# A hybrid trunk layer on one core: new costs and a new waiting rule in the model that orders the projection stage

## The chip, the cores and the metric

One core of a Trainium2 chip runs the whole layer as one program. The metric is the device time of one execution in microseconds (us), from a few repeated runs; smaller is better. The engines are TensorE (PE in the profile: matmul, with its weight loads as PEld), VectorE (DVE), ScalarE (ACT), GpSimd (POOL) and SyncE (SP, which here only issues transfers).

## The reference, cut to what matters

The input is one sequence of 512 frames with 1024 channels. The layer normalizes it, multiplies it by one wide input matrix, and feeds the columns to two recurrent token mixers of eight heads each, which are merged and added back; then an expert retrieval follows, which the change does not touch.

```python
h = _rmsnorm(x, norm1[l])
proj = h @ w_in[l]
a_q, a_k, a_v, a_beta, a_alpha, a_gate, b_f, b_i, b_q, b_gate, g_a, g_b = _split_cols(proj)
...
o_a = _gated_delta_rule(qa, ka, va, beta, log_alpha)
o_a = _rmsnorm(o_a, a_onorm[l]) * jax.nn.silu(a_gate.astype(f32)).reshape(bsz, t, A_HEADS, A_DV)
y_a = o_a.reshape(bsz, t, A_V).astype(dt) @ w_branch_a[l]
...
o_b = _hgrn2_recurrence(qb, 1.0 - f_gate, ib, jnp.log(f_gate))
o_b = _rmsnorm(o_b, b_onorm[l]) * jax.nn.sigmoid(b_gate.astype(f32)).reshape(bsz, t, B_HEADS, B_DV)
y_b = o_b.reshape(bsz, t, B_V).astype(dt) @ w_branch_b[l]
mix = jax.nn.sigmoid(g_a) * y_a + jax.nn.sigmoid(g_b) * y_b
x = x + mix @ w_out[l]
```

Branch A (gated DeltaNet) inverts one triangular 128x128 matrix for each head and each of four chunks; branch B (HGRN2) builds its decayed attention matrix level by level. Both carry a state from chunk to chunk.

## The kernel before, in words

**Units.** The input matrix is cut into units of 128 output columns. A unit is 24 matmuls of 512 columns: eight blocks of the contraction, and for each block three products, since both operands are split into a high and a low float32r part (`piece`: `whi*hhi`, `wlo*hhi`, `whi*hlo`). The high part of the weights is made by ScalarE (L265, tile `whi`), the low part by GpSimd (L470, tile `wlo`, a subtraction of 128x1024 elements that reads two tiles in SBUF). `order` lists the units head by head, with eight kinds for each head (a_k, a_q, b_q, a_v, b_f, b_i, b_gate, a_gate) and some units of the merge gates among them. The first five are done ahead of the stage in question; the next 73 are its projections. After a unit's matmuls `consume` turns it into what the branches need: the causal convolution on VectorE (L922, three taps of 511, 510 and 509 columns), gates (L932, L938, L949), a scan (L940).

**Branches.** Four more generators share the stage with the projections. `setup` runs once. `branch_a1` prepares a head of branch A: it normalizes and transposes keys and queries, makes `LT` (L651) and `AT`, scales keys on GpSimd (`kG` L674, `kd` L675), and inverts 16x16 blocks in 15 small steps on GpSimd (L691, L693). `branch_a2` finishes the inverse on TensorE (`iv`), carries the state and writes `ogA` (L803). `branch_b` runs seven levels for each head; a level is one subtraction of 512 columns on VectorE (L822, tile `z`), two exponentials of 256 columns on ScalarE, two products of 256 columns on VectorE (L826, L827), and then matmuls from `z` into `pl`: in each of the first five levels 16 of them, 640 in all for eight heads. The next level's `z` is written out ahead of a level's matmuls.

**What sets the order.** Every engine carries out its instructions in the order in which the program writes them. In this stage that order is made when the program is built. Each generator stops at a `yield` ahead of a TensorE step and names the tiles that the step reads or writes; the projections stop after each block of three matmuls. A class `Flow` keeps a clock for each engine: after each step `note` goes through the instructions just written, and for each one takes the engine's clock, the time at which its inputs are ready (plus a constant for the pair of engines, `wait`) and the time at which its output buffer is free; the end is that start plus `cost`, a duration by engine, operation and size. The loop then takes the step that could start first on TensorE:

```python
when = max(when, flow.pe()) + BIAS[ch[2]]
if best is None or when < best[0]:
    best = when, ch
```

`BIAS` favours `setup` by 600 ns, `branch_a2` by 100 and `branch_a1` by 50; `branch_b` and the projections have none. So a branch step that the model holds to be ready goes first, and one that it holds to be late lets three projection matmuls go ahead of it. The model decides nothing but this order. On the chip the engines wait for each other by semaphores, whatever the model held. Projections may run ahead of a branch by two heads at most (`allowed`), since the buffers of each kind are two.

After the stage two more merge-gate units and the units of the branch matrices follow in a fixed order, then the expert retrieval.

Of the kernel before, what the change touches and what calls it, by code (L numbers as in the profile page):

```python
# [11 lines left out]
F32R = mybir.dt.float32r  # L12
# [8 lines left out]
PSUM = bass.MemoryType.PSUM  # L21
# [113 lines left out]
class Flow:  # L135


    def __init__(self, nc):
        self.nc, self.pos = nc, 0
        self.eng, self.ready, self.used, self.slots, self.last = {}, {}, {}, {}, {}  # L140
        self.dma, self.ln = 0.0, False

    def keys(self, ap):

        if hasattr(ap, "bass_ap"):
            ap = ap.bass_ap
        elif not hasattr(ap, "tensor"):
            return []
        if ap.tensor.space != bass.MemoryType.SB or not hasattr(ap.tensor, "tag"):
            return [(ap.tensor.name, 0)]  # L150
        dims = [list(d) for d in ap.ap]
        lo = ap.offset % dims[0][0] if dims[0][0] else ap.offset
        hi = lo + sum(max(d[0], 0) * (d[1] - 1) for d in dims[1:])
        return [(ap.tensor.name, q) for q in range(lo // 128, hi // 128 + 1)]

    def cost(self, ins, e, op):
        out = ins.outs[0].bass_ap
        n = out.free_size()
        src = ins.ins[0].bass_ap if len(ins.ins) and hasattr(ins.ins[0], "bass_ap") else out
        psum = any(getattr(a.bass_ap, "space", None) == PSUM for a in ins.ins if hasattr(a, "bass_ap"))  # L160
        if e == "PE":
            w = ins.ins[1].bass_ap
            m = w.free_size()
            if src.dtype == F32:
                if ins.is_transpose:
                    return 112
                return 2 + 0.84 * max(m, n) if n <= 64 and m <= 64 else max(215, 4 * n / 2.4)
            return max(n / 2.4, m * (0.84 if src.dtype == F32R else 0.42)) + 3
        if e == "Activation":
            return 51 + 0.833 * n + (90 if psum else 0)  # L170
        if e == "DVE":
            r = 0.75 if op in ("TensorCopy",) else 1.04
            if src.dtype in (BF16, F16) and out.dtype in (BF16, F16):
                r = 0.53
            return 67 + r * n + (58 if psum else 0)
        if e == "Pool":
            if "pow" in str(ins):
                return 958
            return 100 + {"TensorCopy": 3.45, "TensorScalarPtr": 4.5, "Memset": 0.9}.get(op, 2.05) * n
        return 60  # L180

    def note(self):
        ins_list = self.nc.cur_bb.bb.instructions
        for ins in ins_list[self.pos:]:
            e = str(ins.engine).split(".")[-1]
            if not len(ins.outs) or not hasattr(ins.outs[0], "bass_ap"):
                continue
            t = self.eng.get(e, 0.0)
            ins_k = [k for ap in ins.ins for k in self.keys(ap)]
            out_k = [k for ap in ins.outs for k in self.keys(ap)]  # L190
            for k in ins_k:
                if k in self.ready:
                    r, re = self.ready[k]
                    if r + self.wait(re, e) > t:
                        t = r + self.wait(re, e)
            for ap in ins.outs:
                ten = ap.bass_ap.tensor
                tag = getattr(ten, "tag", None)
                if tag is not None:
                    seen = self.slots.setdefault(tag, [])  # L200
                    if ten.name not in seen:
                        seen.append(ten.name)
                        b = ten.tag_meta.bufs
                        if len(seen) > b and self.last.get(seen[-1 - b], 0.0) + 150 > t:
                            t = self.last[seen[-1 - b]] + 150
            for k in out_k:
                if self.used.get(k, 0.0) > t:
                    t = self.used[k]
            op = str(ins.opcode).split(".")[-1]
            if "DMA" in op:  # L210
                self.eng[e] = t + 60
                n = ins.outs[0].bass_ap.nbytes
                n = n() if callable(n) else n
                self.dma = max(self.dma, t + 1100) + n / 360.0
                end = self.dma
                w = "dma"
            else:
                end = t + self.cost(ins, e, op)
                if op == "Activation" and str(ins.func).split(".")[-1] in ("Ln", "Exp", "Tanh"):
                    ln = str(ins.func).endswith("Ln")  # L220
                    end += 1283 * (ln != self.ln)
                    self.ln = ln
                self.eng[e] = end
                w = e
            for k in out_k:
                self.ready[k] = end, w
            for k in ins_k + out_k:
                self.used[k] = max(self.used.get(k, 0.0), end)
                self.last[k[0]] = max(self.last.get(k[0], 0.0), end)
        self.pos = len(ins_list)  # L230
# [1564 lines left out]
```

## Time and profile before

| | us |
|---|---|
| median of three runs | 2124.62 |
| the three runs | 2121.92, 2124.62, 2127.04 |
| the profiled execution, device time | 2124.58 |
| its span, first to last instruction | 2122.8 |
| PE busy | 2043.1 |
| DVE busy | 1452.4 |
| ACT busy | 937.3 |
| POOL busy | 1160.5 |

The span is what the trace covers. Times below are counted from its start. In this trace a matmul's record is longer than its turn on the engine, since matmuls are pipelined; turns are read from the number of matmuls in a stretch. A float32 matmul leaves two records, a float32r or bfloat16 one leaves one. A row of the view of waits gives the total time that an engine stood idle for another one, the number of such waits and the longest.

### The profile page before, as it was taken

Reading aid. Unit: us, or ns where it says so; the run is one execution under the profiler, and the core shown is the slowest. Engines: PE = TensorE matmul, PEld = TensorE weight load, DVE = VectorE, ACT = ScalarE, POOL = GpSimd, SP = SyncE. Lnnn points to the kernel's source line nnn. Section 1 sums busy time; section 2 is a strip of 40 time slices with the busy share of each in tenths; the row PEclk is TensorE's granted clock in tenths of the full one; section 3 lists DMA queues with packets and bytes.
Section 4 is the critical chain, followed back from the end, with each engine's and each line's share of the span. In section 5 each row is a group of like instructions: output and inputs, shape, how many; then the busy total and the mean of one; then the engine's idle time right before and its main releaser. Section 6 shows DMA issues by size and latency. Waiting matters only on the chain. (4 is left out here: it accounts for less than half of the span.)

```text
span 2122.8 us, 34908 instructions
## 1 busy us (share of the span) xinstructions
PE 2043.1 (96%) x13210; PEld 1753.1 (83%) x13210; DVE 1452.4 (68%) x2779; ACT 937.3 (44%) x1742; POOL 1160.5 (55%) x957
## 2 busy tenths in 40 slices
PE   7899999999999999999789999999999999999997
PEld 5678787787787888889778999999999999999776
DVE  7666646556653366999996666676666676666897
ACT  5555555555554323666575333333333333333233
POOL 3556645655654644211101666666667666666787
PEclk9999999999999999999999999999999999999999
DMA  3313132221212543678799988889888888888775
GB/s 132 116 57 111 52 97 72 82 76 62 92 61 92 198 153 129 184 199 199 195 344 315 322 305 302 303 291 317 298 303 304 291 304 311 304 298 287 246 263 211
DMA packets 189463, 439.44 MB, mean 207 GB/s; under 512 B 26960, under 2 KB 90608, under 8 KB 187632
## 3 DMA queue, kind: packets, MB, share of 16 engines
q1 hardware_dynamic: 95248, 230.75, 31.8%
q0 software_dynamic: 42912, 156.26, 23.5%
q10 hardware_dynamic: 51136, 50.22, 7.1%
q8 instruction: 103, 1.69, 0.3%
q14 instruction: 64, 0.52, 0.1%
HBM read 375.81 MB, written 39.34 MB: 196 GB/s over the span
## 5 line engine op out<-in xcount | busy, mean ns | idle before, releaser
L470 POOL TENSOR_TENSOR wlo<-wraw,whi 128x1024 fp32r<-128x1024 f32 x204 | 501.5, 2458 | 304.3 <-ACT whi L265 296.8
L262 PE MATMUL h<-hhi,wlo 128*128 128x384 f32 x1024 | 347.0, 339 | 6.9 <-DMA wlo<-wraw 6.8
L262 PE MATMUL h<-hhi,whi 128*128 128x384 f32 x1024 | 347.7, 340 | 2.8 <-ACT hext L265 2.8
L262 PE MATMUL h<-hlo,whi 128*128 128x384 f32 x1024 | 346.6, 339 | 1.5 <-POOL hlo L435 1.1
L262 PE MATMUL mm<-hhi,whi 128*128 128x512 f32 x792 | 330.3, 417 | 0.0
L262 PE MATMUL mm<-hlo,whi 128*128 128x512 f32 x792 | 312.4, 394 | 4.2 <-POOL hlo L435 3.0
L1686 DVE TENSOR_TENSOR wl<-hg,wh 128x384 fp32r<-128x384 f32 x126 | 129.7, 1029 | 269.2 <-ACT wh L265 251.2
L262 PE MATMUL mm<-hhi,wlo 128*128 128x512 f32 x792 | 310.6, 392 | 0.7 <-POOL wlo L470 0.7
L265 ACT ACTIVATE whi<-wraw 128x1024 fp32r<-128x1024 f32 (+1 forms) x251 | 263.4, 1049 | 106.4 <-PE mm L262 52.3
L262 PE MATMUL y<-vh,wl 128*128 128x512 f32 x756 | 298.7, 395 | 0.6 <-DVE wl L1686 0.6
L262 PE MATMUL y<-vh,wh 128*128 128x512 f32 x756 | 295.1, 390 | 3.1 <-ACT wh L265 3.1
L262 PE MATMUL y<-vl,wh 128*128 128x512 f32 x756 | 297.1, 393 | 0.9 <-POOL vl L1687 0.9
L1609 POOL DMA_INDIRECT row<-eu,eidx x128 | 158.5, 1239 | 145.6 <-DVE stage L1615 130.7
L1609 POOL DMA_INDIRECT row<-ev,eidx x128 | 161.2, 1260 | 126.1 <-DVE stage L1623 101.2
L265 ACT ACTIVATE hext<-h 128x384 f32<-128x384 f32 x88 | 43.1, 490 | 375.7 <-PE h L262 374.5
L262 PEld LDWEIGHTS h<-hhi,wlo 128*128 128x128 f32 x1024 | 193.7, 189 | 12.3 <-DMA wlo<-wraw 8.4
L262 PEld LDWEIGHTS h<-hhi,whi 128*128 128x128 f32 x1024 | 193.7, 189 | 7.5 <-ACT hext L265 3.5
L262 PEld LDWEIGHTS h<-hlo,whi 128*128 128x128 f32 x1024 | 193.6, 189 | 2.4 <-POOL hlo L435 1.8
L1623 DVE SCALAR_TENSOR_TENSOR stage<-row,stage 128x1024 f32<-128x1024 f32 x127 | 192.6, 1517 | 0.6
L1615 DVE CUSTOM_DVE_ANT_0 stage<-row,h2g 128x1024 f32<-128x1024 f32 x128 | 183.1, 1430 | 0.7
L262 PEld LDWEIGHTS mm<-hlo,whi 128*128 128x128 f32 x792 | 149.2, 188 | 40.4 <-POOL hlo L435 4.7
L262 PEld LDWEIGHTS mm<-hhi,whi 128*128 128x128 f32 x792 | 149.6, 189 | 25.8
(431 smaller groups left out, 3682.2 us busy)
## 6 DMA issues: line engine op xcount, KB each, us to landing
wraw<-eut SPq DMA_DIRECT2D x128, 512.0 KB
stage<-ev SPq DMA_DIRECT2D x126, 512.0 KB
wraw<-wu SPq DMA_DIRECT2D x119, 512.0 KB
stage<-gD ACTq DMA_DIRECT2D x31, 768.0 KB
gD<-stage ACTq DMA_DIRECT2D x11, 2048.0 KB
wlo<-wraw POOLq DMA_DIRECT2D x42, 512.0 KB
sg<-sgD SPq DMA_DIRECT2D x16, 256.0 KB
sgD<-tmpP SPq DMA_DIRECT2D x14, 256.0 KB
```

Source lines behind the costliest of these rows:

```text
L262: nc.tensor.matmul(o, l, r, start=start, stop=stop)
L265: nc.scalar.activation(o, i, f, **kw)
L470: eng.tensor_tensor(lo, raw, hi.bitcast(F32), OP.subtract)
L1609: gps.indirect_dma_start(out=r, out_offset=None, in_=I["eu" if k < P else "ev"], in_offset=bass.IndirectOffsetOnAxis(ap=eidx[:, kk:kk + 1] ...
L1615: vec.tensor_tensor_reduce(out=junk, in0=r, in1=h2g, scale=1.0, scalar=0.0, op0=OP.mult, op1=OP.add, accum_out=hd[:, k:k + 1])
L1623: vec.scalar_tensor_tensor(yg, r, wgt[:, k - P:k - P + 1], yg, OP.mult, OP.add)
L1686: vec.tensor_tensor(wl, hg, wh.bitcast(F32), OP.subtract)
```

## The change

Only the class `Flow` changes, that is, the costs with which the order is made, and so the order of the steps in the stage. No instruction is added or removed, and no size changes.

- TensorE: a float32r matmul costs 0.443 ns a column, 226.8 for 512, in place of 216.3, and the first float32r matmul after another type costs 90 ns more; a float32 matmul costs twice the larger of 27 ns and 0.875 ns a column (54 for 16 or 32 columns, where it was 15 or 29; 224 for 128, where it was 215); a transpose costs 110 in place of 112.
- ScalarE: an activation with a tensor as scale or bias costs 100 ns more, one that also sums its output 200 more. All others keep 51 ns + 0.833 a column, and 90 more from PSUM.
- GpSimd: 180 ns + 2.15 a column for most operations, in place of 100 + 2.05; a power costs 1008 in place of 958.
- VectorE: the costs stay, but a new function `shared` looks at the last 40 GpSimd operations of 512 or more columns that touch no PSUM. A VectorE instruction without PSUM operands whose time overlaps one of these starts at that one's end.

```diff
@@ Flow.cost
+            rounded = src.dtype == F32R
+            again = 90 if rounded and not self.rounded else 0
+            self.rounded = rounded
             if src.dtype == F32:
                 if ins.is_transpose:
-                    return 112
-                return 2 + 0.84 * max(m, n) if n <= 64 and m <= 64 else max(215, 4 * n / 2.4)
-            return max(n / 2.4, m * (0.84 if src.dtype == F32R else 0.42)) + 3
+                    return 110
+                return 2 * max(27, 0.875 * max(m, n))
+            return max(n * 0.443, m * (0.84 if rounded else 0.42)) + again
         if e == "Activation":
-            return 51 + 0.833 * n + (90 if psum else 0)
+            return 51 + 0.833 * n + (90 if psum else 0) + (100 if len(aps) > 1 else 0) + (200 if len(ins.outs) > 1 else 0)
...
             if "pow" in str(ins):
-                return 958
-            return 100 + {"TensorCopy": 3.45, "TensorScalarPtr": 4.5, "Memset": 0.9}.get(op, 2.05) * n
+                return 1008
+            return 180 + {"TensorCopy": 3.45, "TensorScalarPtr": 4.5, "Memset": 0.9}.get(op, 2.15) * n
...
+    def shared(self, ins, e, t, end):
+
+        if e not in ("DVE", "Pool") or any(getattr(a.bass_ap, "space", None) == PSUM for a in list(ins.ins) + list(ins.outs)
+                                           if hasattr(a, "bass_ap")):
+            return t
+        if e == "Pool":
+            if ins.outs[0].bass_ap.free_size() >= 512:
+                self.held.append((t, end))
+                del self.held[:-40]
+            return t
+        for s0, s1 in self.held:
+            if s0 < end and t < s1:
+                t, end = s1, end + s1 - t
+        return t
@@ Flow.note
-                end = t + self.cost(ins, e, op)
+                d = self.cost(ins, e, op)
+                end = self.shared(ins, e, t, t + d) + d
```

## Rows read from the trace of the kernel before

**Rows 1.** The page: the span.
```profile
span 2122.8 us, 34908 instructions
```
**Rows 2.** Windows: busy time by engine (times instructions), granted clock, DMA share, GB/s.
```profile
58.00:698.00 640.00, 618.28 (x5703) 501.78 (x5702) 363.11 (x616) 330.49 (x864) 355.52 (x452) 0.99 0.26 82
...
750.00:800.00 50.00, 50.00 (x222) 41.42 (x221) 35.35 (x32) 13.99 (x16) 23.18 (x10) 1.00 0.46 158
```
**Rows 3.** Waits of TensorE, 58 to 698 us: total us, times, longest.
```profile
PE pl L262 <- DVE z L827: 6.5, 6, 1.8
PE mA L542 <- ACT kT L265: 2.3, 2, 2.1
...
PE iv L262 <- DVE XT L735: 2.2, 4, 1.3
...
PE poB L542 <- ACT vt L265: 1.6, 1, 1.6
...
PE mC L262 <- DVE ga L584: 1.3, 1, 1.3
```
**Rows 4.** Timeline, VectorE and GpSimd, 396 us: start, us, engine, line.
```profile
396.31 2.83 DVE L827 TENSOR_TENSOR z<-z,b_q 128x256 f32<-128x256 f32 x1
...
396.50 2.36 POOL L470 TENSOR_TENSOR wlo<-wraw,whi 128x1024 fp32r<-128x1024 f32 x1
```
**Rows 5.** Timeline, TensorE: five waits, in brackets the idle time before.
```profile
327.89 0.27 PE L262 MATMUL pl<-z 128*32 128x16 f32 x3 [0.71 <-DVE z L827]
...
399.20 0.27 PE L262 MATMUL pl<-z 128*32 128x16 f32 x3 [1.66 <-DVE z L827]
...
552.80 0.27 PE L262 MATMUL pl<-z 128*32 128x16 f32 x3 [1.67 <-DVE z L827]
...
606.05 0.38 PE L262 MATMUL mA<-a_q,kT 128*128 128x128 f32 x1 [0.75 <-DVE LT L651]
...
632.25 0.30 PE L262 MATMUL pl<-z 128*32 128x16 f32 x4 [0.44 <-DVE z L827]
```
**Rows 6.** Forms on VectorE, 58 to 698 us: busy us, mean ns, idle before.
```profile
L922 DVE SCALAR_TENSOR_TENSOR tmpP<-a_k,convw,tmpP 128x511 f32<-128x511 f32 x7 | 13.0, 1864 | 14.2 <-ACT a_k L265 14.2
...
L904 DVE TENSOR_TENSOR tmpB<-poB,r2b 128x512 f32<-128x512 f32 x8 | 5.5, 692 | 21.9 <-POOL r2b L375 21.9
L922 DVE SCALAR_TENSOR_TENSOR tmpP<-a_k,convw,tmpP 128x509 f32<-128x509 f32 x7 | 5.2, 748 | 0.2
```
**Rows 7.** Windows after two of the waits, columns as in rows 2.
```profile
399.00:405.00 6.00, 5.80 (x76) 4.78 (x77) 3.69 (x10) 1.64 (x5) 5.06 (x13) 0.72 0.00 0
552.00:558.00 6.00, 5.20 (x47) 4.18 (x48) 4.31 (x10) 1.65 (x5) 5.21 (x12) 0.72 0.00 0
```
**Rows 8.** Forms on TensorE, 58 to 698 us.
```profile
L262 PE MATMUL mm<-hhi,whi 128*128 128x512 f32 x577 | 245.8, 426 | 0.0
L262 PE MATMUL mm<-hlo,whi 128*128 128x512 f32 x576 | 227.2, 395 | 0.0
...
L262 PE MATMUL pl<-z 128*32 128x16 f32 x1280 | 35.4, 185 | 6.5 <-DVE z L827 6.5
```
**Rows 9.** Forms on ScalarE, 58 to 698 us.
```profile
L265 ACT ACTIVATE z<-z 128x256 f32<-128x256 f32 x112 | 41.2, 416 | 102.8 <-DVE z L822 86.6 <-PE mm L262 9.8 <-PE pl L262 6.3
...
L265 ACT ACTIVATION_READ_ACCUMULATOR junk<-mA 128x1 f32 x60 | 12.8, 213 | 0.0
```
**Rows 10.** Forms on GpSimd, 58 to 698 us.
```profile
L470 POOL TENSOR_TENSOR wlo<-wraw,whi 128x1024 fp32r<-128x1024 f32 x74 | 177.3, 2396 | 190.6 <-ACT whi L265 190.2
```
**Rows 11.** Timeline, VectorE and GpSimd, 650 us.
```profile
650.24 0.69 DVE L822 TENSOR_TENSOR z<-b 128x512 f32<-128x512 f32 x1
650.73 2.44 POOL L470 TENSOR_TENSOR wlo<-wraw,whi 128x1024 fp32r<-128x1024 f32 x1 [3.81 <-ACT whi L265]
```
**Rows 12.** Timeline, the stage's end: last VectorE step of branch A, last unit's consumer.
```profile
688.34 0.75 DVE L803 SCALAR_TENSOR_TENSOR ogA<-mC,vecs,a_gate 128x512 f32<-128x512 f32 x1 [0.76 <-PE mC L542]
...
697.88 0.60 ACT L265 ACTIVATE tmpP<-mm 128x512 f32<-128x512 f32 x1 [3.84 <-PE mm L262]
```

More of the change, by code (lines that the diff above doesn't have):

```diff
@@ L141, in __init__ @@
         self.dma, self.ln = 0.0, False
+        self.rounded, self.held = False, []
     def keys(self, ap):
@@ L159, in cost @@
         src = ins.ins[0].bass_ap if len(ins.ins) and hasattr(ins.ins[0], "bass_ap") else out
-        psum = any(getattr(a.bass_ap, "space", None) == PSUM for a in ins.ins if hasattr(a, "bass_ap"))
+        aps = [a.bass_ap for a in ins.ins if hasattr(a, "bass_ap")]
+        psum = any(getattr(a, "space", None) == PSUM for a in aps)
         if e == "PE":
```

## The prediction

> **What bounds the kernel now.** I read the page first: the span is 2122.8 us [rows 1], and the device time of that execution, 2124.58, is the median of the three runs to 0.04 us. So the sum is made against 2124.6 with nothing to correct. Then I looked for the stretch that the change can touch. The order that it remakes runs from about 58 us, where the loop over the generators begins, to 698 us, where the last projection's result is read [rows 12]. Everything later keeps its order, and I count it as unchanged.
>
> In that stretch the view of windows shows TensorE busy for 618.28 of 640 us [rows 2]; VectorE, ScalarE and GpSimd are busy little more than half of it. TensorE bounds the stage, and 640 - 618.28 = 21.7 us is all that it stood still. The view of waits says for whom: its twelve rows hold 25 waits and sum to 21.5 us, of which the five shown are the ones I argue with [rows 3]. Branch B's `z` alone makes 6.5 us in six waits. No row of the twelve names a transfer. So the prize is small from the start: at the very most some 25 us of 2125, and what matters is which waits the new costs can foresee.
>
> The timeline shows the mechanism behind the largest group. At 396.31 us VectorE takes up a product of 256 columns (L827), and it lasts 2.83 us, because GpSimd is on a 2.36 us subtraction from 396.50 on [rows 4]; the two end together at about 399, and TensorE, which the order had already brought to that head's `pl` matmuls, stands idle for 1.66 us [rows 5]. The forms view shows that this is the rule and not an accident: the first convolution tap has a mean of 1864 ns and the third, one or two columns shorter, 748, while an operation that reads PSUM takes 692 [rows 6]. The model of before knows nothing of it.
>
> **The change, part by part.** No instruction is added or removed, so each part is worth what it does to TensorE's 21.5 us of waits, to what follows from them, and to the number of times TensorE changes between matmul types.
>
> *VectorE waits for GpSimd (`shared`).* Five waits of the list have this cause by the timeline: before 327.89, 399.20, 552.80, 606.05 and 632.25, with 0.71, 1.66, 1.67, 0.75 and 0.44 us of idle time [rows 5], 5.2 us together. With the rule the model holds these products to be late and lets projection blocks go first, which exist in plenty. Bounds: 0 to 5.2 us gained; I take 5.2, since the GpSimd subtractions behind four of them are the weight splits, written out at the start of a unit and so known to the model when the product is priced.
>
> *The clock.* After two of these waits the granted clock over 6 us is 0.72 [rows 7], that is, part of the stretch ran at the lower of the two levels, 1.2 GHz. That costs 6 x 0.28 = 1.7 us each, 3.4 us. In both cases TensorE had stood idle for 1.7 us just before. If the waits go, so should these: bounds 0 to 3.4, I take 3.4.
>
> *TensorE's, ScalarE's and GpSimd's durations.* A projection matmul takes 50.00 / 222 = 225 ns by the trace [rows 2]; the old cost was 216.3, the new one is 226.8. A 16-column `pl` matmul takes 35.4 us / 640 = 55 ns [rows 8]; old 29, new 54. The first matmul after a change of type is visible too: `whi` matmuls of `hhi`, which begin each block, have a mean of 426 ns and the last of a block 395 [rows 8], which is 31 x 577 = 17.9 us, or some 200 changes at 90 ns. The old model took none of this into account, and ran TensorE's clock too fast by about 15 us in float32r matmuls (8.7 ns x 1730), 18 in changes and 17 in `pl` matmuls alone. The second row that the model lacked is ScalarE's read of an accumulated sum, 213 ns [rows 9], which is now priced at 200; GpSimd's split takes 2396 ns [rows 10], old cost 2199, new 2382.
>
> What are these worth? Of the 16.3 us of waits that are left, 2.0 belong to `setup` (the largest is `ga`, 1.3 [rows 3]), which the bias of 600 ns sends ahead on purpose; they stay. The other 14.3 us come from ScalarE and VectorE queues that were later than planned, such as the 2.3 us for `kT` and the 2.2 for `XT` [rows 3]. Bounds 0 to 14.3; I take half, 7.1, because costs that remain as they were (a ScalarE half of `z`, 264 by the formula and 416 by the trace [rows 9]) lie in the same queues.
>
> *New waits.* The old model's TensorE was too fast, and this had a good side: TensorE came back to a branch later than planned, which covered costs that were too small elsewhere. With true TensorE costs that cover is gone. For `z` the shortfall is 2 x (416 - 264) = 304 ns a level, and there are 112 / 2 = 56 levels [rows 9]. TensorE comes back in blocks of three matmuls, 3 x 225 = 675 ns, so if the moment falls anywhere in a block the mean wait is 304 x 304 / (2 x 675) = 68 ns, and 3.8 us over all levels. Bounds: 0, and 56 x 0.304 = 17.0 us; I take 3.8.
>
> *Changes of type.* Each filled wait may split a run of matmuls: 25 x 90 ns = 2.2 us at most, none at least; I take 1.1.
>
> *The end of the stage, and VectorE held too long in the model.* What the trace shows also speaks against the rule: at 650.24 a subtraction on VectorE starts 0.49 us ahead of a GpSimd split and takes 0.69 us, undisturbed [rows 11]; the new function would put it behind the split, some 2.4 us late. The Trainium skill ("SBUF — State Buffer", "Who interferes with whom") says that issue order decides who blocks: whoever starts first holds the shared ports for a whole instruction, and VectorE instructions with one SBUF input outside the two-port modes do not contend at all. By that page the function is right in rows 4 and too dark in rows 11, and there the trace agrees. What does a branch step cost that is placed too late? Nothing to TensorE while projections remain. They remain to the end: branch A's last VectorE step starts at 688.34 and the last unit's result is read at 697.88 [rows 12], 9.5 us of cover. If head 7's chain slipped by more, the rest would be idle time. In its last 75 us some nine splits lie (74 in 640 us [rows 10]), so at most 9 x 2.4 = 22 us of lateness and 12 of loss. Bounds 0 to 12; I take 0. Transfers move with their steps on SP's queue, and the splits on GpSimd's; as no wait of TensorE names a transfer, I cost this at nothing, covered by the same projections.
>
> The sum: -5.2 - 3.4 - 7.1 + 3.8 + 1.1 = -10.8 us, which gives 2113.8; I say 2114.
>
> **The rivals.** *The waits only change place.* The order is remade from the first step on, so every meeting of a VectorE product and a GpSimd split falls elsewhere, and small costs that stay wrong make new waits of the same total. For it: ScalarE's and VectorE's plain costs are untouched. Against it: the two largest errors of the model are mended. It gives 2120.4 to 2128.8, most likely 2124. To it belongs the case that the function finds little to hold, because operations under 512 columns, or such as are written later, escape it.
>
> *TensorE comes too early.* One mechanism on the slower side: with TensorE priced in full and ScalarE's halves of `z` still 152 ns short each, the order returns to `pl` before `z` at nearly every level. For it: the shortfall is in the rows, at 56 places. Against: of the 56 only six waited before. Price: 17.0 us of new waits, the 5.2 and 3.4 still gained and nothing of the others: 2124.6 + 17.0 - 8.6 = 2133. It makes the kernel slower once TensorE's new waits for `z` exceed 8.6 + 4.2 = 12.8 us, 0.23 us a level.
>
> **How the numbers follow.** A measurement of this kernel tells about 0.2% (4.2 us) from no change. Forecast, faster: 0.60, with a range of its own from 2104 to 2120. Waits only change place: 0.22. Too early: 0.18. The low end takes all waits but `setup`'s and both dips, 19.5 + 3.4 = 22.9 us: 2102. The high end goes most of the way to the slower rival: 2131.
>
> **What would show it.** In the changed kernel TensorE's waits in the stage should fall from 21.5 to some 12 us, with none over 1 us for a `z` that GpSimd held up; no stretch of the stage should show a granted clock near 0.72; and the stage should end near 687 in place of 698, with everything behind it shifted alike. The block's first matmul should keep a mean near 426 ns. The forecast is wrong if the sum of waits stays near 21 us, or if rows such as `pl` waiting for `z` grow many and short. It would be wrong in another way if branch A's last step came after the last projection.

## The result and the profile after

The changed kernel takes 2110.49 us (median of six runs, 2108.85 to 2111.22), the kernel before 2123.12 in the same series (six runs). The ratio is 0.9938, with a 95% interval from 0.9925 to 0.9951: 12.6 us less, where 10.8 were forecast. The profiled execution took 2111.22 us, its span 2109.3 against 2122.8 [rows 1].

Where the time went is read best at one point behind the stage: the start of ScalarE's reading of the last merge-gate unit, just ahead of the branch matrices. First the timeline of before there, then that of after:

```profile
715.03 0.60 ACT L265 ACTIVATE sg<-mm 128x512 f32<-128x512 f32 x1 [5.01 <-DVE mA L1131]
```

```profile
702.42 0.60 ACT L286 ACTIVATE sg<-mm 128x512 f32<-128x512 f32 x1 [5.00 <-DVE mA L1152]
```

So 12.6 of the span's 13.5 us are gone by then. Below is the view of TensorE's waits after, from 58 us to that point (who waits, at which line, for whom; total us, times, longest), which answers to [rows 3]:

```profile
PE mA L563 <- ACT kT L286: 3.8, 4, 1.7
PE trb L625 <- DVE g L402: 1.8, 1, 1.8
PE mC L283 <- DVE SA L811: 1.4, 2, 0.8
PE mA L283 <- DVE AT L685: 1.2, 2, 0.8
PE iv L283 <- ACT XT L286: 1.0, 1, 1.0
PE mC L590 <- DVE tmpA L586: 0.7, 1, 0.7
PE mm L283 <- ACT a_k L286: 0.6, 1, 0.6
PE mA L283 <- ACT dec L286: 0.6, 1, 0.6
PE mC L563 <- DVE tmpA L821: 0.5, 1, 0.5
...
PE poB L563 <- DVE tmpB L889: 0.3, 1, 0.3
```

The eleven rows sum to 12.3 us, 9.2 less than before, and the six waits of `pl` for `z`, the 6.5 us at the head of the list of before, are gone altogether. The windows of that stretch (columns as in [rows 2]) and the forms on TensorE and VectorE say what else there is to see:

```profile
58.00:702.42 644.42, 631.04 (x5776) 513.25 (x5774) 369.52 (x621) 337.45 (x877) 364.47 (x459) 1.00 0.28 89
```

```profile
L283 PE MATMUL mm<-hhi,whi 128*128 128x512 f32 x592 | 250.1, 422 | 1.0 <-ACT a_k L286 0.6 <-ACT tmpP L286 0.4
L283 PE MATMUL mm<-hlo,whi 128*128 128x512 f32 x592 | 232.6, 393 | 0.0
...
L283 PE MATMUL pl<-z 128*32 128x16 f32 x1280 | 35.4, 185 | 0.0
```

```profile
L943 DVE SCALAR_TENSOR_TENSOR tmpP<-a_k,convw,tmpP 128x511 f32<-128x511 f32 x7 | 12.1, 1733 | 10.0 <-ACT a_k L286 10.0
...
L943 DVE SCALAR_TENSOR_TENSOR tmpP<-a_k,convw,tmpP 128x509 f32<-128x509 f32 x7 | 5.2, 749 | 0.2
```

The granted clock is 1.00 in the whole stretch: the two dips of before [rows 7], 1.7 us each, are absent. 9.2 us of waits and 3.4 of clock make 12.6. VectorE was not relieved: its first tap still takes 1733 ns and its third 749, as in [rows 6]. GpSimd holds it up as before; TensorE only has something else to do meanwhile. One such place, from the timeline after: a half of `z` takes 2.88 us beside a split, and TensorE goes through projection matmuls from 476.25 to past 479.

```profile
475.91 2.88 DVE L848 TENSOR_TENSOR z<-z,b_q 128x256 f32<-128x256 f32 x1
```

```profile
476.12 2.38 POOL L491 TENSOR_TENSOR wlo<-wraw,whi 128x1024 fp32r<-128x1024 f32 x1
```

```profile
476.25 0.50 PE L283 MATMUL mm<-hhi,whi 128*128 128x512 f32 x1
```

Last, the end of the stage, which answers to [rows 12] (timeline, ScalarE and VectorE):

```profile
684.09 0.60 ACT L286 ACTIVATE tmpP<-mm 128x512 f32<-128x512 f32 x1 [2.31 <-PE mm L283]
```

```profile
685.25 0.75 DVE L824 SCALAR_TENSOR_TENSOR ogA<-mC,vecs,a_gate 128x512 f32<-128x512 f32 x1 [0.75 <-PE mC L563]
```

The last projection is now read 1.2 us ahead of branch A's last step, where it was 9.5 us behind it. The cover at the end is used up, at a price of 0.5 us (the wait for `tmpA`).

### The profile page after: what moved, and what is told of

Read it like the earlier page. It is cut to its first block, busy times and chain, and to the rows that moved or that the text cites. A ratio compares the mean times of both kernels' runs of the same rounds, so it can differ in the third digit from the quotient of the medians.

```text
span 2109.3 us, 34910 instructions
## 1 busy us (share of the span) xinstructions
PE 2039.1 (97%) x13210; PEld 1751.5 (83%) x13210; DVE 1450.8 (69%) x2779; ACT 936.4 (44%) x1742; POOL 1155.1 (55%) x957
## 3 DMA queue, kind: packets, MB, share of 16 engines
q0 software_dynamic: 42912, 156.26, 23.7%
## 5 line engine op out<-in xcount | busy, mean ns | idle before, releaser
L283 PEld LDWEIGHTS h<-hhi,wlo 128*128 128x128 f32 x1024 | 193.7, 189 | 13.5 <-DMA wlo<-wraw 9.5
L283 PEld LDWEIGHTS mm<-hhi,whi 128*128 128x128 f32 x792 | 149.0, 188 | 27.6 <-ACT a_k L286 1.0
```

The costliest lines, as they stand in the source:

```text
L283: nc.tensor.matmul(o, l, r, start=start, stop=stop)
```

## The experiments

Twelve kernels ran. To compare them I made the same account for each: when the last merge-gate unit is read; all waits of TensorE from 58 us to there; of these the waits of `pl` for `z`; and what the clock lost, as the sum over windows of 10 us of 1 less the granted clock, times the window (idle time inside a dip counts in both). Differences to before are the medians' within one series.

| kernel | to before, us | ratio, 95% interval | unit read at | waits (count) | of them for z | clock lost | reading less both |
|---|---|---|---|---|---|---|---|
| before | | | 715.0 | 21.5 (24) | 6.5 | 3.4 | 690.1 |
| changed | -12.6 | 0.9925 to 0.9951 | 702.4 | 12.3 (16) | 0 | 0 | 690.1 |
| e1, rule alone | +9.6 | 1.0035 to 1.0060 | 725.0 | 28.2 (32) | 2.2 | 8.5 | 688.3 |
| e2, durations alone | +12.4 | 1.0048 to 1.0074 | 726.4 | 34.0 (40) | 12.4 | 0 | 692.4 |
| e3, TensorE's alone | +40.8 | 1.0182 to 1.0208 | 753.1 | 49.4 (55) | 11.8 | 5.1 | 698.6 |
| e4, narrow rule | +6.3 | 1.0017 to 1.0041 | 723.3 | 23.2 (26) | 1.8 | 10.3 | 689.8 |
| e5, ScalarE corrected | +13.4 | 1.0052 to 1.0080 | 729.3 | 29.1 (29) | 1.4 | 13.6 | 686.6 |
| e6, one more unit | -10.9 | 0.9938 to 0.9965 | 701.8 | 11.8 (15) | 0 | 0 | 690.0 |
| e7, mean in place of rule | +3.2 | 1.0007 to 1.0025 | 720.4 | 23.5 (21) | 3.5 | 10.2 | 686.7 |
| e8, e4 and e6 | +1.7 | 1.0002 to 1.0020 | 720.1 | 22.3 (23) | 2.0 | 10.2 | 687.6 |
| e9, 1.5 ns on TensorE | +4.9 | 1.0014 to 1.0034 | 720.9 | 22.9 (20) | 0 | 8.5 | 689.5 |
| e10, 10 ns on GpSimd | -0.7 | 0.9984 to 1.0002 | 714.4 | 20.2 (23) | 0 | 5.1 | 689.1 |
| e11, before with 2 ns | +9.7 | 1.0033 to 1.0060 | 722.7 | 27.6 (29) | 6.0 | 3.4 | 691.7 |
| e12, branch A favoured | +7.9 | 1.0022 to 1.0046 | 723.1 | 23.7 (26) | 2.0 | 8.5 | 690.9 |

The last column is the point of the account: but for e3 it stays within 6 us, while the readings spread over 28. So an order costs mainly its waits and its dips. In e3 some 8 us more are in neither, and what they are is not shown.

**e1: the waiting rule alone.** The new `shared`, all costs as before.

```diff
-            again = 90 if rounded and not self.rounded else 0
+            again = 0
...
-                    return 110
+                    return 112
-                return 2 * max(27, 0.875 * max(m, n))
+                return 2 + 0.84 * max(m, n) if n <= 64 and m <= 64 else max(215, 4 * n / 2.4)
-            return max(n * 0.443, m * (0.84 if rounded else 0.42)) + again
+            return max(n / 2.4, m * (0.84 if rounded else 0.42)) + 3
...
-            return 180 + {"TensorCopy": 3.45, "TensorScalarPtr": 4.5, "Memset": 0.9}.get(op, 2.15) * n
+            return 100 + {"TensorCopy": 3.45, "TensorScalarPtr": 4.5, "Memset": 0.9}.get(op, 2.05) * n
```

> The waiting rule alone, with all costs of before. My theory, that the rule removes the five waits behind GpSimd (5.2 us) and with them the two clock dips (3.4 us): no wait of pl for a z that GpSimd held, no dip in the stage, about 8.6 us less, some 2114.5 us. Rival, that the rule is worth little while the model's TensorE clock runs too fast: waits for z stay at several us and the time is above 2119. Rival, that any new order scatters the waits: the sum of waits stays near 21 us, of another make.

Measured: 9.6 us slower than before; no one of the three comes as put. The waits for `z` do fall, from 6.5 to 2.2 us, and neither of the two that are left follows a step that GpSimd held up; but waits of another make take their place, and more, 28.2 us where the last rival had 21. The largest rows of its waits:

```profile
PE mC L563 <- DVE tmpA L821: 6.1, 3, 4.0
PE mC L283 <- DVE SA L811: 4.1, 6, 2.3
PE iv L283 <- DMA X<-XD: 3.8, 3, 2.1
PE pl L283 <- DVE z L848: 2.2, 2, 1.1
```

All but the last are branch A's own chain, and the timeline puts one of them at the stage's end: 3.95 us before 705.52, when no projection is left to fill it (the last one is read at 691.40, branch A ends at 706.43).

```profile
698.00 0.49 PE L283 MATMUL mC<-vb,XT 128*128 128x128 f32 x2 [0.22 <-DVE SA L811]
700.01 0.49 PE L283 MATMUL mC<-vb,XT 128*128 128x128 f32 x2 [0.22 <-DVE SA L811]
705.52 0.87 PE L563 MATMUL mC<-ident,tmpA 128*128 128x128 f32 x4 [3.95 <-DVE tmpA L821]
```

I read it so, though no run shows it by itself: a later VectorE against a TensorE that is priced too fast makes the branches late twice over; projections go first too often and run out.

**e2: the durations alone.**

```diff
-                end = self.shared(ins, e, t, t + d) + d
+                end = t + d
```

> All new durations, without the waiting rule. My theory: the waits behind GpSimd come back, three to six of them of up to 1.8 us in front of pl, 5 to 8 us slower than the changed kernel, some 2117 us, and a dip or two if such a wait falls badly. Rival, that the durations do the whole work: within 2 us of the changed kernel, 2110.5.

Measured: 12.4 us slower than before, 25 slower than the changed kernel. The waits behind GpSimd come back as my theory had it: by the timelines five of the fifteen waits for `z`, 4.7 us, follow a half of `z` that a split held up (over 1 us in place of 0.42). The size is not the theory's. The other ten, 7.7 us, follow halves that nothing held, and 25 more waits are for other tiles.

```profile
PE pl L283 <- DVE z L848: 12.4, 15, 1.4
PE pl L283 <- ACT tmpB L286: 2.8, 1, 2.8
PE mA L283 <- DVE LT L672: 2.6, 1, 2.6
```

**e3: of the durations only TensorE's.** As e2, and the costs of ScalarE and GpSimd as before.

```diff
-            return 51 + 0.833 * n + (90 if psum else 0) + (100 if len(aps) > 1 else 0) + (200 if len(ins.outs) > 1 else 0)
+            return 51 + 0.833 * n + (90 if psum else 0)
...
-            return 180 + {"TensorCopy": 3.45, "TensorScalarPtr": 4.5, "Memset": 0.9}.get(op, 2.15) * n
+            return 100 + {"TensorCopy": 3.45, "TensorScalarPtr": 4.5, "Memset": 0.9}.get(op, 2.05) * n
```

> Of the change only TensorE's durations. TensorE's clock in the model is then right and the other engines' costs as small as before. If the cover theory holds (a TensorE that is priced too fast hides costs that are too small elsewhere), the waits of TensorE in the stage rise above the 21.5 us of before, most of them for z and for what ScalarE reads, and the time is above 2124. Rival, that true TensorE durations help by themselves: waits under 17 us, time below 2119.

Measured: 40.8 us slower than before. This fits the cover theory: 49.4 us of waits, and they stand in front of what VectorE and ScalarE write for both branches.

```profile
PE pl L283 <- DVE z L848: 11.8, 17, 1.3
PE mA L563 <- DVE a_v L947: 8.5, 6, 2.1
PE mC L283 <- ACT vn L286: 4.7, 3, 1.6
PE pl L283 <- DVE a L878: 3.6, 3, 1.6
```

The corrections that [rows 2] and [rows 8] give most directly, TensorE's, are by themselves the worst kernel of all.

**e4: a narrower rule.** VectorE waits in the model only when it would start inside a GpSimd operation.

```diff
-            if s0 < end and t < s1:
+            if s0 <= t < s1:
```

> The changed kernel, but a VectorE instruction waits in the model only where it would start inside a GpSimd operation, not where it starts ahead of one. If lateness in the model eats the cover at the stage's end, branch A's last step comes earlier than 685.25 us and the time falls by 1 to 2 us, to some 2109. If the broader rule is needed (a product whose start is misjudged by little is still held up), waits for z come back and the time is 2 to 5 us longer than 2110.5.

Measured: 6.3 us slower than before, and so 19 over the changed kernel, far outside both expectations. Waits for `z` return by 1.8 us only, and 1.7 of these follow a `z` that nothing held. The rest is the end of the stage and the clock: behind 640 us TensorE waits 4.0 us for `tmpA`, branch A ends at 704.58, the last projection is read at 692.22, and the window there shows a lower clock as well.

```profile
690.00:712.00 22.00, 16.36 (x78) 13.11 (x77) 2.14 (x4) 4.95 (x17) 3.91 (x5) 0.84 0.25 83
```

I had expected the narrower rule to bring branch A forward, and it came 19 us later. It is also what the Trainium skill would make of the rule ("SBUF — State Buffer", "Who interferes with whom": issue order decides who blocks). The trace does not bear this out by the starts of its records. In e4's own trace a half of `z` starts at 167.54, 0.21 us ahead of a split, and still takes 2.86 us, as the one in [rows 4] does with a lead of 0.19; the narrow rule lets both through. In the changed kernel a subtraction at 245.28 with a lead of 0.15 us ran undisturbed in 0.68, and the split took 2.76 in place of some 2.4. So the starts of the records alone do not say which of the two is held.

**e7: the mean in place of the rule.**

```diff
-            return 67 + r * n + (58 if psum else 0)
+            return 67 + r * n + (58 if psum else 245 if n >= 256 else 0)
...
-                end = self.shared(ins, e, t, t + d) + d
+                end = t + d
```

> The new durations without the waiting rule; instead every VectorE operation of 256 or more columns without PSUM is priced 245 ns higher, which is 78.7 us, the time that VectorE was held up in the stage before, over its 320 such operations. Theory of foresight: the rule works because it knows which product is late; with the mean alone the waits behind GpSimd come back, TensorE waits for z for 4 us or more, and the time lies 5 to 12 us above the changed kernel, 2116 to 2123. Rival, balance: what counts is that branches are held to be late enough against a true TensorE clock; then the waits for z vanish too and the time is within 3 us of 2110.5.

Measured: 2127.66 us, 3.2 over before, somewhat beyond the range of the theory of foresight. The waits for `z` lie between both theories, three of 3.5 us in sum, where e2 had fifteen. Two of the three, 2.2 us, follow a half that GpSimd held, where e2 had five of 4.7 us and the changed kernel none. So a mean lateness does part of the rule's work in this one order; the clock took 10.2 us in it.

**e5: ScalarE as the trace shows it.** On top of the changed kernel.

```diff
-            return 51 + 0.833 * n + (90 if psum else 0) + (100 if len(aps) > 1 else 0) + (200 if len(ins.outs) > 1 else 0)
+            return (151 if psum else 130) + 0.833 * n + (100 if len(aps) > 1 else 0) + (200 if len(ins.outs) > 1 else 0)
```

> The changed kernel with ScalarE priced as the trace shows it: 130 ns + 0.833 a column from SBUF and 151 + 0.833 from PSUM, in place of 51 and 141 (a split of 1024 columns is then 983, a half of z 343). If what is left of the waits comes from costs that are too small, the waits for what ScalarE writes (kT 3.8, XT 1.0, a_k 0.6, dec 0.6 us) fall by half and the time goes to some 2108. Rival, the end of the stage: branch A's last step already comes 1.2 us after the last projection is read; more lateness in the model empties the end, idle time appears behind 660 us, and the time rises by 3 to 10 us.

Measured: 13.4 us slower than before. The rival has the direction, and the idle end that it named: TensorE waits 7 us behind 660 us. Its 3 to 10 us were too small, for durations nearer to the trace give a kernel 26 us slower than the changed one, with 16.8 us more of waits and 13.6 lost to the clock. The projections end early (690.86), branch A late:

```profile
709.90 0.75 DVE L824 SCALAR_TENSOR_TENSOR ogA<-mC,vecs,a_gate 128x512 f32<-128x512 f32 x1 [1.21 <-PE mC L563]
```

**e6: one more unit in the stage.** With its two loads moved.

```diff
-NPROJ = 64 + 14
+NPROJ = 64 + 15
...
         last, obs = None, {}
+        early(NPROJ + 1)
```

> The changed kernel with one more merge-gate unit inside the stage (79 units in place of 78; the two loads that this needs earlier are moved with it). It gives the end of the stage 5.4 us more cover. In the changed kernel the wait there is 0.5 us, so the cover is worth at most about 1 us: 2109.5 to 2111. A gain of over 2 us would say that the end costs more than TensorE's waits show.

Measured: 2113.58 us, 2.6 over the expected range; it is 0.9951 of before, and its interval overlaps that of the changed kernel. The wait at the end of the stage is gone, the unit is read 0.7 us earlier, and the next stage takes it back: up to 740 us TensorE waits longer for `mA`, 2.9 us, where the changed kernel waits 0.8.

```profile
PE mm L283 <- DVE mA L1152: 2.9, 2, 2.1
```

**e8: the narrower rule with the one more unit.** Both edits as above.

> The narrower rule of the fourth run (wait only when starting inside) with the one more unit inside the stage. In the fourth run TensorE stood idle for 5.6 us behind 640 us, where branch A's last step came 12 us after the last projection was read. If the empty end is its cause, the unit fills most of it: the idle time there falls by 4 us or more and the time from 2129.8 to some 2124 or below (more if the clock's dips near 626 and 711 us go too). If the time stays, the loss lies elsewhere.

Measured: 2126.21 us; to before it is 4.6 us better than e4. The 4 us less of idle time behind 640 us that I expected did not come: TensorE's waits there went from 5.1 to 4.2 us, branch A's last step still comes 5.5 us after the last projection is read, and the wait for `tmpA` is whole. The unit did not fill the end, so what a filled end is worth in this order stays open.

```profile
PE mC L563 <- DVE tmpA L821: 4.2, 1, 4.2
```

**e9 and e10: a difference that means nothing.** On the changed kernel, 1.5 ns more for a float32r matmul; or 10 ns more for a GpSimd operation, where the split of 1024 columns is priced 2382 and takes 2396 by [rows 10].

```diff
-            return max(n * 0.443, m * (0.84 if rounded else 0.42)) + again
+            return max(n * 0.446, m * (0.84 if rounded else 0.42)) + again
```

> The changed kernel with a float32r column priced 0.446 ns in place of 0.443, which is 1.5 ns a matmul and less than the trace can tell from the truth. If the gain is owed to a model that is right, the time stays within 3 us of 2110.5. If an order is a draw that any small difference makes anew, the time is some other value between 2105 and 2135, with waits and clock dips of another make.

```diff
-            return 180 + {"TensorCopy": 3.45, "TensorScalarPtr": 4.5, "Memset": 0.9}.get(op, 2.15) * n
+            return 190 + {"TensorCopy": 3.45, "TensorScalarPtr": 4.5, "Memset": 0.9}.get(op, 2.15) * n
```

> The changed kernel with GpSimd's constant 190 ns in place of 180, the same question on another engine, which only makes branch steps later by 10 ns for each GpSimd operation. Right model: within 3 us of 2110.5. Draw: anywhere between 2105 and 2135.

Measured: e9 4.9 us slower than before, e10 the same as before. Both lose the whole gain. Yet in both no `pl` waits for `z` at all. What they lose is elsewhere; the largest rows of e9, then of e10:

```profile
PE mA L563 <- ACT kT L286: 4.9, 3, 2.4
PE poB L283 <- ACT SB L286: 4.8, 2, 2.9
PE mC L563 <- DVE tmpA L821: 4.0, 1, 4.0
```

```profile
PE mA L563 <- ACT kT L286: 4.5, 5, 2.1
PE mC L563 <- DVE tmpA L821: 4.0, 1, 4.0
PE iv L283 <- DMA X<-XD: 1.9, 2, 1.6
```

In both branch A's last step comes after the last projection is read (by 13.9 and 6.4 us), with the same 4.0 us wait at the end, and the clock dips. Here is e10's clock, three of the windows of 10 us:

```profile
448.00:458.00 10.00, 7.93 (x56) 6.09 (x55) 5.49 (x9) 6.06 (x18) 3.54 (x3) 0.83 0.16 47
518.00:528.00 10.00, 8.86 (x122) 7.38 (x123) 6.11 (x6) 3.94 (x13) 6.00 (x4) 0.83 0.43 132
688.00:698.00 10.00, 5.86 (x27) 4.82 (x26) 1.79 (x3) 2.85 (x11) 3.91 (x5) 0.85 0.24 79
```

**e11: the same question on the kernel before.**

```diff
-            return max(n / 2.4, m * (0.84 if src.dtype == F32R else 0.42)) + 3
+            return max(n / 2.4, m * (0.84 if src.dtype == F32R else 0.42)) + 5
```

> The kernel before with 2 ns more for each float32r matmul in its model (5 in place of 3), which is 2 of the 9 ns that it lacks. Draw: the time differs from before by several us either way. Otherwise it stays within 3 us, or goes up by a fifth of what TensorE's durations alone cost, 8 us, if cover is lost in proportion.

Measured: 9.7 us slower than before, for 2 ns a matmul. Its interval, 7.0 to 12.7 us, takes in the 8 us of the proportional cover, so the time does not tell that from a draw. The waits grew by 6.1 us, none of it in front of `z` (6.0, six times). Which of the two it is stays open; it is one neighbour of before, and slower.

**e12: branch A favoured.**

```diff
-BIAS = (-600, -100, -50, 0, 0)
+BIAS = (-600, -300, -150, 0, 0)
```

> The changed kernel with branch A favoured more: 300 and 150 ns in place of 100 and 50. Branch A's last step then comes earlier than 685 us and the end of the stage has cover again; each of its 200 and more steps may make TensorE wait up to 0.2 us longer. If the end is what limits the changed kernel, the time falls below 2109; if waits grow, it rises by 2 to 10 us, with many short waits for what branch A reads.

Measured: 7.9 us slower than before and some 20 over the changed kernel, twice what I allowed for growing waits. The waits nearly doubled, to 23.7 us, the clock lost 8.5, and branch A's last step came later than in the changed kernel, at 701 us, not earlier.

No version beats the changed kernel.

## Why the prediction was right, and where its reasons were not

*The bound and the sum.* The prize was TensorE's waits and the dips after them, 25 us at most (the view of [rows 3] has 24 waits, not 25; nothing hangs on it). This held: the account closes for before and after to 0.1 us (690.1 both). The marks named ahead came too: 12.3 us of waits (12 forecast), a full clock, the last projection read at 684 (687), a first matmul of 422 ns (426).

*The rule.* Forecast: five waits behind GpSimd gone, 5.2 us. All are gone, and with them a sixth that I had left among the others, the longest for `z`. Before 100.22 us the subtraction that opens a level took 2.88 us beside a split, where one takes 0.68 undisturbed, and both halves of `z` came late by it. So this term measured 7.0 us. From the timeline of before:

```profile
95.44 2.85 POOL L470 TENSOR_TENSOR wlo<-wraw,whi 128x1024 fp32r<-128x1024 f32 x1
```

```profile
95.94 2.88 DVE L822 TENSOR_TENSOR z<-b 128x512 f32<-128x512 f32 x1
```

```profile
100.22 0.23 PE L262 MATMUL pl<-z 128*32 128x16 f32 x2 [1.81 <-DVE z L827]
```

And this part alone does not depend on the draw. The seven kernels with the full rule keep 0 to 2.2 us of waits for `z`, the two with the narrow one 1.8 and 2.0, the four without it, before among them, 6.0 to 12.4; with the mean in its place 3.5 are left. The timelines say more. In every kernel between 8 and 17 of the 168 subtractions and halves of `z` took over 1 us, each beside a GpSimd operation: 13 before, 14 after. In the four kernels without the rule 53 such steps were followed by 26 waits of TensorE for that `z`, 24.4 us; in the seven with the full rule 95 by two, 1.4 us, both in e12. The narrow rule had two in 20 (0.5 us), the mean two in 13 (2.2 us). GpSimd holds up as many steps as ever, and TensorE is no longer there to wait for them: the rule does what the prediction said.

Two readings beside it were wrong. I called the function right in [rows 4] on the ground that whoever starts first holds the ports, but there VectorE's product starts 0.19 us ahead of the split and is held all the same; only [rows 11] fits. And there the function would make the subtraction 2.9 us late (650.24 to 653.17), not 2.4, which takes the bound of the end of the stage from 12 to some 17 us.

*The clock.* Forecast 3.4 us, measured 3.4. But the step "if the waits go, so should these" holds for these two dips only. Most other orders have dips, at other waits, up to 13.6 us of them; that none fell into the changed kernel's stage is 5.1 of the 12 us by which it leads e10.

*The durations and the new waits.* Forecast: 7.1 us of the other waits removed, 3.8 new ones. Their balance, -3.3 us, was measured as -4.0 (16.3 us of other waits before, 12.3 after), or -2.2 when the sixth wait is put to the rule. As separate terms they failed. I added parts that do not add: alone the rule costs 9.6 us and the durations 12.4, together they save 12.6. The loss of cover that true TensorE durations bring was put too small without the rule: I bounded it by 17.0 us, all in front of `z`, and e3 shows 28 us more waits than before, of which `z` has only 5. With the rule and the new costs of ScalarE and GpSimd, which make the branches later again, this loss does not appear. That the rule supplies the lateness that true TensorE durations take away fits e1 to e3, but it is argued and not shown: e7 supplies as much lateness as a mean and is still 3.2 us over before.

*Changes of type.* Forecast +1.1 us; the mean excess of a block's first matmul went from 31 ns to 29, over the same 592 blocks 18.4 to 17.2 us, which the rounding of the means alone could make. The +1.1 did not show.

*The end of the stage.* I took 0 of a bound of 12 us, on 9.5 us of cover. The price was 0.5 us, but the cover was not there any more: branch A's last step comes 1.2 us after the last projection is read, which I had named as a sign of being wrong in another way. Here the mechanism failed, and that the price was small is luck. In e1, e4, e5, e8, e9 and e10 branch A's last step follows the last projection, and TensorE stands idle for about 4 us for `tmpA`. The risk that I put at nothing there is real. So is that of transfers, which I put at nothing too: none is waited for in the changed kernel, but e1 waits 3.8 us for `X` by DMA and e10 1.9.

*The rivals.* "The waits only change place" had 0.22. It describes e10, 10 ns away, with 20.2 us of waits and none of them for `z`. "TensorE comes too early" is what e2 and e3 do. That the forecast's size came out is in good part luck: this one order has few waits of any kind, and nothing that I read ahead of the result could tell that from e9's or e10's. Of the ten orders made with the rule, the narrow rule or the mean, two are faster than before (the changed one and e6, which is the same order but for its end), one is the same and seven are slower. Where the changed order differs from its neighbours is settled (waits, end, dips); why a constant as small as e10's leads there is open: which of the swapped steps makes the extra waits was not tried.

## What to carry to other kernels

The order that this greedy model writes out is in good part a draw: before a gain of half a per cent is put down to a better model, change a constant by less than its error and run again. Do not expect a truer cost on one engine to help by itself: the two slowest kernels here, e3 and e5, each put one engine nearer to the trace, and with e3 the likely reason is slack that its other costs had needed. And look at the end of such a stage first, where the filler runs out.

## What had not been expected of the hardware

Neither the sum nor the length of TensorE's waits tells whether the clock dips. e2 has 40 waits of 34.0 us in all, the longest 2.8, and its stretch keeps the full clock; e7 has 21 waits of 23.5 us, the longest 2.3, and lost 10.2 us at the lower level. In before itself the waits of 1.66 and 1.67 us are followed by a dip [rows 7], and the 1.81 us before 100.22 are not. Windows of e2, then two of e7:

```profile
58.00:726.42 668.42, 632.97 (x5774) 510.84 (x5772) 361.34 (x621) 340.28 (x876) 370.32 (x459) 1.00 0.27 86
```

```profile
128.00:138.00 10.00, 7.44 (x55) 5.72 (x56) 4.70 (x6) 6.49 (x21) 3.34 (x3) 0.66 0.65 213
598.00:608.00 10.00, 8.68 (x64) 6.86 (x65) 8.04 (x10) 5.92 (x18) 6.21 (x4) 0.66 0.59 199
```

A window at 0.66 costs 3.4 us, as much as two long waits. So orders with nearly equal waits can lie far apart: e4 has 1.7 us more waits than before, loses 6.9 us more to the clock, and reads the unit 8.2 us later.
